# Layer norm over channels: 1/std spread by a store and a broadcast load instead of TensorE, its sums in a one-bank PSUM accumulator, and a new table for the planned order

## The chip, the cores and the metric

One NeuronCore of a Trainium2 chip runs the whole program. The metric is the time of one execution on the device in microseconds (us); a figure for a kernel is the median over its runs. TensorE does matmuls, VectorE and ScalarE elementwise work, GpSimd some elementwise work and DMA issues, SyncE only issues DMAs.

## The reference

One layer of a decoder on 1024 tokens of 1024 channels, then a final RMSNorm, all in float32. Cut to what matters:

```python
h = rmsnorm(x, norm_g) * (1.0 + scale) + shift
u = h @ w_in                                   # 5 groups of 1024 columns
cv, cg, cs, lx, ls = split(u)
v = cv * sigmoid(cg)
v = causal_depthwise_conv(v, dw_w, dw_b)       # 31 taps
v = silu(layernorm(v, cln_g, cln_b))           # over the 1024 channels
v = v @ pw2_w + pw2_b
y_conv = v * silu(cs)
...                                            # y_lru from lx, ls: conv, gates, scan
y = concat([y_conv, y_lru]) @ w_out
x = x + (1.0 + gate) * y
return rmsnorm(x, final_g)
```

with `layernorm(v) = (v - mu) * rsqrt(var + eps) * g + b`, where `mu` and `var` are taken over the channels of a token.

## The kernel before, in words

**Layout.** Channels lie on the 128 partitions, in 8 tiles, and the 1024 tokens in the free dimension. So a sum over channels is a sum over the partitions and over 8 tiles, and a number per token (a mean, a 1/std) has to be spread over the partitions before VectorE can use it. A float32 matmul operand is split into a high and a low part in the type fp32r, and a product is three matmuls of 128x512: `uh,whi`, `ul,whi` and `uh,wlo` (`mm_k`, line 739). Where two column tiles or two row tiles are taken together, sums and differences of their blocks save products (`duo` for two tiles of W_in with the accumulators `up` and `dn`; `lru_pair` for two column tiles of W_out with `lx`, `lw`, `lc`, `ld`; `pair_products` for the projection pw2, with `xpw`, `ypw`, `zpw`, and for the rest of W_out, with `xout`, `yout`, `zout`).

**Stages.** RMSNorm of x with the modulation; the 40 column tiles of W_in in the order of the string `ORDER`, with the depthwise convolution of a value tile as soon as that tile is there, and gates and scan of the lru group between; then the lru half of W_out, which needs no layer norm; the layer norm over channels beside it; pw2; the conv half of W_out; the final norm. The conv outputs are eight tiles `c` (four go through DRAM and come back as `cr`), their sum is `csum`.

**The layer norm** (`layer_norm`, line 1735). `csum` is split in `csh` and `csl`, and a matmul with ones spreads the mean over the partitions (`mean`, line 1742). VectorE subtracts the mean from each tile, ScalarE squares it into `lnsq`, VectorE adds the squares up in `lnss`. Then `rstd` (line 957) does three steps: eight matmuls with a column of ones (line 970) sum `lnss` over the partitions into 8 columns of the PSUM tile `lnbc`, token by token down the partitions; ScalarE takes the root (`sd`), VectorE the reciprocal (`rs`, line 987); and eight matmuls with the identity (line 976) turn the 128x8 numbers into a 128x1024 tile in which every partition has every token's 1/std. VectorE multiplies each tile by `lnbc` out of PSUM, ScalarE applies scale, bias and Silu. VectorE and ScalarE then make the operands of pw2 out of them: `vha`, `vhb`, `vhc` and `vhT` are high parts of tiles, sums and differences, `vla`, `vlb` and so on their low parts. The weights of pw2 come as `rawpw` loads on SyncE's queue and are split into `whipw`, `wlopw`, `h34pw`, `l34pw`, `hlpw`.

**What sets the order.** Every instruction is handed to a planner (`Plan`, line 334) with its engine, a cost, a priority and the tiles that it reads and writes. `Plan.order` walks through time with these costs, takes for each free engine the ready operation with the smallest priority whose tiles are to be had, and so fixes the order on each engine; `Plan.run` adds to the priorities the numbers of the table `TURNS`, which name an engine, the first and the last tile of an operation and its count:

```python
seen[key] = n = seen.get(key, -1) + 1
o.prio += TURNS.get((*key, n), 0.0)
out = self.order()
```

The engines run their lists in order. SyncE's list is the queue of the ordinary loads and stores, so a DMA that waits for its data holds up all DMAs behind it. Constants choose who does a piece of work: `WE` and `DENG` give the low parts of weights to VectorE, GpSimd or a DMA that adds, `CENG` sums of the convolution, `LRV` the remainders of the lru weights.

**Memory.** 47 big tiles of 128x1024 in SBUF; two each of the weight tiles `raw`, `whi`, `wlo`; in PSUM three tiles `mm` of two banks and two tiles `acc` of one bank (128x512). `lnbc` and `mean` are `mm` tiles, and so are the accumulators of the W_in and W_out products.

Of the kernel before, what the change touches and what calls it, by code (L numbers as in the profile page):

```python
# [34 lines left out]
ORDER = "i10 i24 i2 g0 i25 i11 i3 i26 i33 i12 i4 g1 i34 i23 g2 i13 i35 i5 i27 g3 i20 i14 i39 i6 i28+i36 i15 i30+i38 i7 i29+i37 g5 i31 g4 i19 i18+i22 g6 i21 g7"  # L35
# [12 lines left out]
HRES = 2  # L48
# [42 lines left out]
KQ = 0.5  # L91
# [64 lines left out]
LRV = (0, 1, 2, 3, 4, 5, 6)  # L156
# [19 lines left out]
WE = {5: "POOL", 6: "DMA", 7: "DVE", 8: "POOL", 9: "POOL", 10: "DVE", 11: "POOL", 12: "POOL", 13: "POOL", 14: "DMA", 16: "POOL", 18: "DVE", 19: "DVE", 20: "DVE", 21: "DVE", 23: "DVE", 24: "DVE", 25: "POOL", 26: "DVE", 27: "POOL", 28: "DMA", 30: "POOL", 31: "DMA", 32: "DMA", 33: "DMA", 34: "DMA", 35: "DVE", 36: "DVE", 37: "DVE", 38: "DVE", 39: "DMA", 40: "POOL", 41: "DVE"}  # L176
PDIRECT = (2, 4, 5, 6, 7)
D1S = {15: -1.35, 18: -1.35, 19: -1.35, 21: -0.3, 22: 0.0, 23: -1.35, 25: -1.35, 26: -1.35, 29: -0.3, 32: -1.35, 33: 0.0, 35: -1.35, 36: -1.35, 38: -1.35, 39: -1.35, 40: 0.0, 41: -1.35}
PGM, PYM, PXL, PYL, PXR = (2, 3), (0, 4), (0,), (4, 6, 7), (4, 6)
# [2044 lines left out]
```

## Time and profile before

| what | before |
|---|---|
| median of 3 runs | 721.93 us (721.25 to 722.73) |
| the profiled execution | 722.32 us, of which the span of instructions 720.5 us |
| TensorE busy | 710.7 us, 99% of the span, 3244 matmul instructions |
| VectorE busy | 642.2 us, 89% |
| ScalarE busy | 475.4 us, 66% |
| GpSimd busy | 217.9 us, 30% |
| DMA | 136.61 MB, mean 190 GB/s |
| mean granted clock of TensorE | 0.996 |

The profiled execution has a time of its own; its span is shorter by what lies ahead of the first and behind the last instruction. A busy share is the time with at least one instruction running on an engine. The matmuls overlap one another: one lasts 389 ns in the records, and the next one starts before it ends, so what a row of matmuls costs is read from start to start. "PE", "DVE", "ACT", "POOL" and "SP" stand for TensorE, VectorE, ScalarE, GpSimd and SyncE; L976 is line 976 of the kernel. An arrow "<-" behind an idle time names what ended it.

### The profile page before, as it was taken

What the parts mean: (1) busy time and instruction counts of PE and PEld (TensorE: products, weight loads), DVE (VectorE), ACT (ScalarE), POOL (GpSimd) and SP (SyncE); (2) the same over time, 40 slices, a digit from 0 to 9 for tenths busy, and PEclk for the clock granted to TensorE, in tenths of its full rate; (3) what the DMA queues carried; (4) which work ended last, traced back from release to release, by engine and by line L of the source; (5) the groups of instructions that cost most, each with busy time, mean ns of one, the idle gap of its engine ahead of it and who ended that gap; (6) DMA issues with size and microseconds to landing.
All of it is one profiled execution on the core that took longest, in us unless ns stands there. A gap on an engine that the chain in (4) does not pass through costs nothing.

```text
span 720.5 us, 9054 instructions
## 1 busy us (share of the span) xinstructions
PE 710.7 (99%) x3244; PEld 591.5 (82%) x3244; DVE 642.2 (89%) x884; ACT 475.4 (66%) x601; POOL 217.9 (30%) x188
## 2 busy tenths in 40 slices
PE   9999999999999999999999999999999999999996
PEld 8888888888888888887788888888888888878885
DVE  7989999899989989969988999999699874998747
ACT  7650699848748865974694979947497654744422
POOL 0023334554765752374163361100111011100001
PEclk9999999999999999999999999999999999999998
DMA  9946358998787999699764339997737855893006
GB/s 336 407 159 192 56 151 198 255 268 184 172 216 198 246 232 230 168 228 200 220 173 117 88 92 275 256 341 196 177 49 151 217 126 129 247 251 116 30 1 233
DMA packets 45196, 136.61 MB, mean 190 GB/s; under 512 B 5104, under 2 KB 14576, under 8 KB 45040
## 3 DMA queue, kind: packets, MB, share of 16 engines
q1 hardware_dynamic: 27440, 90.00, 35.5%
q0 software_dynamic: 16704, 45.13, 35.0%
q10 hardware_dynamic: 1008, 0.92, 0.4%
q8 instruction: 25, 0.41, 0.2%
q14 instruction: 19, 0.16, 0.1%
HBM read 83.30 MB, written 25.69 MB: 151 GB/s over the span
## 4 chain that ended last, share of the span: by engine, by line
PE 84%; DVE 7%; ACT 3%; issue 3%; POOL 2%; DMA 1%; DVEq 0%; POOLq 0%; ACTq 0%
PE ps L747 36%; PE xout L923 5%; PE first L1056 5%; PE xpw L923 5%; PE dn L747 3%; PE lx L1640 3%; PE dn L1851 3%; PE gate L1487 2%; PE ypw L923 2%; PE up L747 2%; DVE caccs L606 1%; PE y L893 1%; DMA wloout<-in_w_out_dram 1%; PE zout L923 1%; PE lx L747 1%
## 5 line engine op out<-in xcount | busy, mean ns | idle before, releaser
L747 PE MATMUL ps<-uh,whi 128*128 128x512 f32 x448 | 138.0, 389 | 0.0
L747 PE MATMUL ps<-uh,wlo 128*128 128x512 f32 x448 | 138.0, 389 | 0.0
L747 PE MATMUL ps<-ul,whi 128*128 128x512 f32 x448 | 137.8, 389 | 0.0
L747 PEld LDWEIGHTS ps<-ul,whi 128*128 128x128 f32 x448 | 84.1, 188 | 17.4
L747 PEld LDWEIGHTS ps<-uh,wlo 128*128 128x128 f32 x448 | 84.1, 188 | 17.4
L747 PEld LDWEIGHTS ps<-uh,whi 128*128 128x128 f32 x448 | 84.0, 188 | 17.4
L606 DVE SCALAR_TENSOR_TENSOR cacc<-v,V,cacc 128x511 f32<-128x511 f32 (+14 forms) x90 | 66.7, 741 | 0.2
L587 ACT CAST whi<-raw 128x1024 fp32r<-128x1024 f32 (+1 forms) x44 | 44.1, 1007 | 33.7 <-issue 11.2
L606 DVE SCALAR_TENSOR_TENSOR caccs<-v,V,caccs 128x511 f32<-128x511 f32 (+6 forms) x84 | 62.5, 744 | 3.7 <-ACT caccs L595 2.8
L606 DVE SCALAR_TENSOR_TENSOR caccs<-c,wsum,caccs 128x511 f32<-128x511 f32 (+6 forms) x84 | 62.4, 743 | 0.7
L614 POOL TENSOR_TENSOR wlo<-raw,whi 128x1024 fp32r<-128x1024 f32 (+1 forms) x16 | 38.6, 2416 | 71.8 <-ACT whi L587 70.1
L595 ACT ACT_TABLE_LOAD x45 | 57.7, 1283 | 3.5 <-DVE r L1499 1.1
L619 POOL DMA_DIRECT2D es<-cq x30 | 28.3, 944 | 27.9 <-DMA es<-cq 11.8
L606 DVE SCALAR_TENSOR_TENSOR modw<-modw,sc 128x1024 f32<-128x1024 f32 x23 | 32.4, 1412 | 0.2 <-DMA modw<-in_mod_w_dram 0.2
L614 DVE TENSOR_TENSOR wlo<-raw,whi 128x1024 fp32r<-128x1024 f32 (+1 forms) x22 | 28.7, 1306 | 2.0 <-ACT whi L587 2.0
L619 POOL DMA_DIRECT2D oo<-co x26 | 26.1, 1067 | 14.4 <-issue 5.5
L595 ACT ACTIVATE cq<-v,V 128x511 f32<-128x511 f32 (+14 forms) x30 | 21.1, 711 | 13.6 <-DVE modw L606 6.5
L619 POOL DMA_DIRECT2D accd<-acc x8 | 7.0, 874 | 72.9 <-ACT acc L595 51.4
L614 POOL TENSOR_TENSOR o<-fin,bc 128x256 f32<-128x256 f32 (+1 forms) x6 | 4.9, 836 | 70.9 <-ACT bc L587 70.9
L595 ACT ACTIVATE finsq<-fin 128x512 f32<-128x512 f32 (+2 forms) x14 | 7.9, 571 | 27.0 <-DVE fin L606 14.8
L619 POOL DMA_DIRECT2D lz<-in_w_out_dram x16 | 14.1, 948 | 37.2 <-ACT lz L595 32.8
L606 DVE SCALAR_TENSOR_TENSOR xs<-ps,V,xs 128x1023 f32<-128x1023 f32 (+2 forms) x15 | 19.2, 1278 | 4.2 <-ACT xs L595 4.1
(523 smaller groups left out, 1928.6 us busy)
## 6 DMA issues: line engine op xcount, KB each, us to landing
raw<-in_w_in_dram SPq DMA_DIRECT2D x36, 512.0 KB, 4.8
modw<-in_mod_w_dram SPq DMA_DIRECT2D x24, 512.0 KB, 8.4
scsd<-scs SPq DMA_DIRECT2D x8, 512.0 KB, 3.6
raw<-in_w_out_dram SPq DMA_DIRECT2D x8, 512.0 KB, 5.2
accd<-acc POOLq DMA_DIRECT2D x8, 512.0 KB, 5.9
rawpw<-in_pw_dram SPq DMA_DIRECT2D x8, 512.0 KB, 4.6
scsr<-scsd SPq DMA_DIRECT2D x8, 512.0 KB, 5.6
rawout<-in_w_out_dram SPq DMA_DIRECT2D x8, 512.0 KB, 4.0
```

What stands on the lines that cost most here:

```text
L587: act.copy(out(), in_())
L595: act.activation(out=out(), in_=in_(), func=func, **kw)
L606: dve.scalar_tensor_tensor(out=out(), in0=in0(), scalar=scalar, in1=in1(), op0=op0, op1=op1, accum_out=accum)
L614: lambda: e.tensor_tensor(out=out(), in0=a(), in1=b(), op=op), prio, r, w,
L619: return S.op("POOL", ISSUE, lambda: pool.dma_start(out(), a(), accum_op=ALU.add), prio, r, w, lag=RATE * n / T, after=after, flight=flight)
L747: pe.matmul(ps()[:, a - off:b - off], k3(lhs)()[:, at, :], rhs[k]()[:, a:b], start=(k == first and lhs is wh and rhs is xh and (a - off) % ...
L893: pe.matmul(to(), half(*lhs)()[:, j * P:j * P + P], half(*rhs)()[:, c0:c1], start=a == "S1" and j == 0 and t == 0, stop=j == KT // 2 - 1 a ...
L923: pe.matmul(half(ps, 0)(), half(*lhs)()[:, j * P:j * P + P], half(*rhs)(), start=start and at == 0 and i == 0, stop=at == len(order) - 1 a ...
L1056: pe.matmul(ps()[:, a - off:b - off], fw_part(lhs, k, i * P, i * P + P)(), rhs()[:, a:b], start=k == 0 and lhs is wh and rhs is xh, stop=k ...
L1487: pe.matmul(ps()[:, c0:c1], lhs()[:, j, :], rhs()[:, c0:c1], start=st == 0, stop=st == 2)
L1640: pe.matmul(half(ps, h)(), lhs()[:, o:o + P], half(*rhs)(), start=begin and at == 0 and t == 0, stop=at == len(order) - 1 and t == len(ter ...
L1851: pe.matmul(half(ps, h)(), lhs()[:, o:o + P], half(rhs, z)(), start=begin and j == 0 and t == 0, stop=j == NJ - 1 and t == 2, skip_group_c ...
```

## The change

The layer norm calls a new function instead of `rstd` with `lnbc`:

```diff
-        bc = mm_tile("lnbc")
-        rstd(-1, [ss], 0, T, bc, 0)
+        if LNB == "PE":
+            bc = mm_tile("lnbc")
+            rstd(-1, [ss], 0, T, bc, 0)
+        else:
+            bc = root_rows(ss, o)
```

```diff
+LNB, LNC, LNP, LNS = "DMA", False, 0.5, "acc"
...
+    def root_rows(ss, last_sq):
+
+
+        sums, rs = (acc_tile if LNS == "acc" else mm_tile)("lnsum"), S.buf("rs", "lnrs")
+        row = dram.tile([1, T], F32, tag="lnrow", name="lnrow")
+
+        def stats():
+            for b in range(KT):
+                pe.matmul(sums()[:, b:b + 1], ss().rearrange("p (t b) -> p b t", b=KT)[:, b, :],
+                          ones[:, 0:1], start=False, stop=True, skip_group_check=True)
+        TS(-1, lambda: sums()[:, :KT], lambda: ones[:, :KT], 0.0, None, ALU.mult, w=[sums], after=[last_sq])
+        S.op("PE", 0.224 * KT, stats, -1, [ss], [sums])
+        ACT(-1, lambda: rs()[:, :KT], lambda: sums()[:, :KT], AF.Sqrt, KT, bias=eps_t, scale=1.0 / D,
+            r=[sums], w=[rs])
+        S.op("DVE", 0.2, lambda: dve.reciprocal(rs()[:, :KT], rs()[:, :KT]), -1, [rs], [rs])
+        DMA(LNP, lambda: row[0].rearrange("(p b) -> p b", b=KT), lambda: rs()[:, :KT], P * KT * 4,
+            r=[rs], w=[("lnrow", 0)])
+        wide = big_buf("lnwide")
+        DMA(LNP, wide, lambda: row.to_broadcast([P, T]), FULL_BYTES, r=[("lnrow", 0)], w=[wide])
+        if not LNC:
+            return wide
...
```

So the eight matmuls of the sums write into a one-bank accumulator (`lnsum`, zeroed by VectorE, then added to), with every eighth token in a column instead of 128 tokens in a row, so that the 8 numbers of a partition lie side by side in memory. Root and reciprocal work in one tile `lnrs`. SyncE stores its 128x8 numbers into a row of 1024 in DRAM (`lnrow`, 32 bytes from each partition) and loads that row into every partition of the SBUF tile `lnwide`. VectorE multiplies by `lnwide` from SBUF. The eight matmuls with the identity are gone.

Beside it the tables that set the order are new: `TURNS` grows from 117 entries to 951, `ORDER` swaps some slots, and a few constants move single pieces of work:

```diff
-ORDER = "i10 i24 i2 g0 i25 i11 i3 i26 i33 i12 i4 g1 i34 i23 g2 i13 i35 i5 i27 g3 i20 i14 i39 i6 i28+i36 i15 i30+i38 i7 i29+i37 g5 i31 g4 i19 i18+i22 g6 i21 g7"
+ORDER = "i10 i24 i2 g0 i25 i11 i3 i26 i33 i12 i4 g1 i34 i23 g2 i13 i35 i5 i27 g3 i20 i39 i14 i6 i28+i36 i15 i30+i37 i7 i29+i38 g4 g5 g6 i31 i19 i22+i18 g7 i21"
...
-LRV = (0, 1, 2, 3, 4, 5, 6)
+LRV = (0, 1, 2, 4, 5, 6)
...
 TURNS = {
...
-    ("ACT", "c1", "cq1_14", 0): -8,
-    ("ACT", "c3", "vhb1", 0): -1.7,
+    ("ACT", "", "", 1): -0.2,
+    ("ACT", "c1", "cq1_10", 0): 0.8,
...
```

(`i` is a column tile of W_in, `+` a duo, `g` a pair of gates of the lru group.) Other constants of the same kind that differ: `HRES`, `KQ`, `DENG`, `EVD`, `DUOE`, `PRES`, `PREP`, `XCP`, `HSP`, `CENG`, `LWO`, `WE`, `PDIRECT`, `D1S`, `PYL`. Over the whole program, TensorE's matmuls of 128x512, 128x256 and 128x1 are the same in number, and those of 128x128 are 8 fewer.

**TensorE at the sums and the spread.** The rows of `lru_pair` on both sides are products of W_out (`yh`, `yl`: lru outputs, `whi`, `wlo`, `lsh`, `lsl`: weights). Before:

```order
L1640 MATMUL lx_4221<-yhs_3858,lsl_4076 128x512
L970 MATMUL lnbc<-ones,lnss 128x1 x8
L747 MATMUL lw_4230<-yh_3368,whi_4155 128x512
L747 MATMUL lw_4230<-yl_3383,whi_4155 128x512
L747 MATMUL lw_4230<-yh_3368,wlo_4163 128x512
L747 MATMUL lw_4230<-yh_3864,whi_4155 128x512
L747 MATMUL lw_4230<-yl_3883,whi_4155 128x512
L747 MATMUL lw_4230<-yh_3864,wlo_4163 128x512
L976 MATMUL lnbc<-ident,rs-1_0_4285 128x128 x8
L1640 MATMUL lx_4221<-yhs_3908,whi_4155 128x512
```

and in the changed kernel:

```order
L2475 MATMUL lc_4251<-yh_3812,whi_4172 128x512
L2475 MATMUL lc_4251<-yl_3859,whi_4172 128x512
L2475 MATMUL lc_4251<-yh_3812,wlo_4212 128x512
L2578 MATMUL lnsum<-ones,lnss 128x1 x8
L2475 MATMUL lc_4251<-yh_3780,whi_4172 128x512
L2475 MATMUL lc_4251<-yl_3790,whi_4172 128x512
L2475 MATMUL lc_4251<-yh_3780,wlo_4212 128x512
```

The sums stand 9 matmuls of 128x512 sooner in TensorE's list, and behind them the W_out products go on with no spread in between.

**VectorE from the last sums of squares to the first product.** `lnss` is the running sum, `ld` and `lw` are sums of W_out blocks in PSUM with a copy `lk`. Before:

```order
L614 TENSOR_TENSOR lnss<-lnss,lnsq_4192 128x1024
L614 TENSOR_TENSOR ld_4253<-lx_4221,lk_4244 128x512
L614 TENSOR_TENSOR lnss<-lnss,lnsq_4219 128x1024
L614 TENSOR_TENSOR lw_4230<-lx_4221,lk_4244 128x512
L987 RECIPROCAL rs-1_0_4285<-sd-1_0_4283 128x8
L614 TENSOR_TENSOR c_3289<-c_3289,lnbc 128x1024
```

and in the changed kernel:

```order
L1463 TENSOR_SCALAR lnsum<-ones 128x8
L1449 TENSOR_TENSOR lnss<-lnss,lnsq_4119 128x1024
L1449 TENSOR_TENSOR lnss<-lnss,lnsq_4189 128x1024
L1449 TENSOR_TENSOR lnss<-lnss,lnsq_4214 128x1024
L1449 TENSOR_TENSOR wlo_4272<-raw_4191,whi_4257 128x1024
L2584 RECIPROCAL lnrs<-lnrs 128x8
L1449 TENSOR_TENSOR ld_4290<-lx_4237,lk_4235 128x512
L1449 TENSOR_TENSOR lw_4219<-lx_4237,lk_4235 128x512
L1449 TENSOR_TENSOR c_2349<-c_2349,lnwide 128x1024
L1449 TENSOR_TENSOR cr_3984<-cr_3984,lnwide 128x1024
```

The zeroing of `lnsum` stands three additions ahead of the sums; the remainder of a W_out weight (`wlo`) and the piece `ld` have come between the last `lnss` and the products, which read `lnwide`.

**SyncE's queue.** `raw` are weights of W_out, `rawpw` those of pw2. Before:

```order
L633 DMA raw_4174<-in_w_out_dram 128x1024
L633 DMA raw_4201<-in_w_out_dram 128x1024
L633 DMA rawpw_0_4371<-in_pw_dram 128x1024
L633 DMA rawpw_1_4386<-in_pw_dram 128x1024
L633 DMA rawpw_0_4581<-in_pw_dram 128x1024
```

and in the changed kernel:

```order
L1468 DMA raw_4191<-in_w_out_dram 128x1024
L1468 DMA lnrow<-lnrs 128x8
L1468 DMA lnwide<-lnrow 128x1024
L1468 DMA rawpw_0_4355<-in_pw_dram 128x1024
L1468 DMA rawpw_1_4358<-in_pw_dram 128x1024
L1468 DMA rawpw_0_4540<-in_pw_dram 128x1024
```

Store and broadcast load stand between the last `raw` and the first `rawpw`, so all loads of pw2's weights are issued behind them.

**TensorE at the start of pw2.** In the changed kernel:

```order
L1582 MATMUL lc_4369<-yh_3828,whi_4257 128x512
L1582 MATMUL lc_4369<-yl_3847,whi_4257 128x512
L1582 MATMUL lc_4369<-yh_3828,wlo_4272 128x512
L1758 MATMUL xpw_0_4531<-vha_4363,whipw_4439 128x512
L1758 MATMUL xpw_0_4531<-vha_4363,wlopw_4455 128x512
L1758 MATMUL xpw_0_4531<-vha_4521,whipw_4439 128x512
L1758 MATMUL xpw_0_4531<-vha_4521,wlopw_4455 128x512
L1582 MATMUL ld_4411<-yh_3371,whi_4257 128x512
```

Before, the 12 products of `ld` with this weight stood ahead of the first `xpw`; now they stand between the first products of pw2, three at a time at first.

## Rows read from the trace of the kernel before

**Rows 1.** The page: busy time; TensorE and its granted clock in 40 slices, in tenths.
```profile
PE 710.7 (99%) x3244; PEld 591.5 (82%) x3244; DVE 642.2 (89%) x884; ACT 475.4 (66%) x601; POOL 217.9 (30%) x188
...
PE   9999999999999999999999999999999999999996
...
PEclk9999999999999999999999999999999999999998
```

**Rows 2.** Waits of PE: who waited for whom, total us, times, longest us.
```profile
PE lx L1640 <- ACT acc L595: 0.4, 1, 0.4
PE xout L923 <- DMA wloout<-in_w_out_dram: 0.4, 1, 0.4
PE dn L1851 <- DVE dn L614: 0.4, 1, 0.4
PE dn L1851 <- ACT up L587: 0.3, 1, 0.3
```

**Rows 3.** Timeline of PE, 507.5 to 508.8 us: start, duration, instruction.
```profile
507.79 0.39 PE L747 MATMUL lx<-yh,wlo 128*128 128x512 f32 x1
508.58 0.50 PE L1640 MATMUL lx<-yh,whi 128*128 128x512 f32 x1 [0.40 <-ACT acc L595]
```

**Rows 4.** The chain that ended last, 486 to 525 us: start, duration, what.
```profile
514.32 1.36 PE lx L1640 x6
515.67 1.68 PE lnbc L970 x16
...
518.87 1.78 PE lnbc L976 x16
520.65 1.39 PE lx L1640 x6
```

**Rows 5.** Timeline of DVE, 513 to 522 us, with idle time ahead.
```profile
513.67 1.22 DVE L614 TENSOR_TENSOR lnss<-lnss,lnsq 128x1024 f32<-128x1024 f32 x1
...
517.69 0.20 DVE L987 RECIPROCAL rs-1_0_4285<-sd-1_0_4283 128x8 f32<-128x8 f32 x1 [1.28 <-ACT sd-1_0_4283 L595]
520.69 2.35 DVE L614 TENSOR_TENSOR c<-c,lnbc 128x1024 f32<-128x1024 f32 x2 [2.79 <-PE lnbc L976]
```

**Rows 6.** Timeline of ACT, 513 to 526 us.
```profile
517.39 0.27 ACT L595 ACTIVATE sd-1_0_4283<-lnbc,eps_t 128x8 f32<-128x8 f32 x1 [3.31 <-PE lnbc L970]
...
521.95 2.38 ACT L595 ACTIVATE c<-c,V 128x1024 f32<-128x1024 f32 x2 [2.98 <-DVE c L614]
```

**Rows 7.** DMA issues: times, KB each, median us to landing.
```profile
rawpw<-in_pw_dram SPq DMA_DIRECT2D x8, 512.0 KB, 4.6
...
rawout<-in_w_out_dram SPq DMA_DIRECT2D x8, 512.0 KB, 4.0
...
lsdl<-ll SPq DMA_DIRECT2D x4, 512.0 KB, 7.1
...
lsl<-lsdl SPq DMA_DIRECT2D x4, 512.0 KB, 7.3
...
out_dram<-o SPq DMA_DIRECT2D x9, 128.0 KB, 2.4
```

**Rows 8.** Timeline of SP's queue, 500 to 560 us.
```profile
509.23 39.27 SPq L633 DMA_DIRECT2D rawpw<-in_pw_dram  x3
```

**Rows 9.** Timeline of PE, 553.1 to 553.3 us.
```profile
552.95 0.39 PE L747 MATMUL ld<-yh,wlo 128*128 128x512 f32 x1
553.17 0.39 PE L923 MATMUL xpw<-vha,whipw 128*128 128x512 f32 x1
```

**Rows 10.** Groups of ACT, 521 to 553 us, by shape: busy us, mean ns.
```profile
L595 ACT ACTIVATE cr<-cr,V 128x1024 f32<-128x1024 f32 x4 | 5.0, 1238 | 0.0
...
L587 ACT CAST vhb<-c 128x1024 fp32r<-128x1024 f32 x3 | 3.1, 1045 | 0.0
...
L587 ACT CAST vha<-cr 128x512 fp32r<-128x512 f32 x3 | 1.8, 628 | 0.0
```

**Rows 11.** Timeline of POOL, 630 to 646 us.
```profile
634.48 0.86 POOL L619 DMA_DIRECT2D wloout<-in_w_out_dram  x1 [4.08 <-ACT wloout L595]
```

More of the change, by code (lines that the diff above doesn't have):

```diff
@@ new lines @@
+    ("ACT", "cacc6", "c6", 0): -0.7,
+    ("ACT", "caccs2", "c2", 0): -1,
+    ("ACT", "caccs7", "c7", 0): -1,
+    ("ACT", "cr0", "lnss", 0): 0.9,
+    ("ACT", "cr0", "vha0", 0): -5,
+    ("ACT", "cr1", "vhb0", 0): 1.7,
+    ("ACT", "cr2", "lnsq2", 0): -1.6,
+    ("ACT", "cr2", "vha1", 0): 4.3,
+    ("ACT", "cr4", "vha2", 0): 6,
+    ("ACT", "dn27", "up27", 0): -0.1,
+    ("ACT", "dn37", "scs2", 0): 0.1,
+    ("ACT", "dn37", "wk37", 0): -1.6,
+    ("ACT", "first_u0", "first_u0", 0): 6.4,
+    ("ACT", "fraw2", "fhi2", 0): -1,
@@ new lines @@
+    ("DVE", "c3", "lnwide", 0): 0.2,
+    ("DVE", "c3", "mean", 0): -10.2,
+    ("DVE", "c3", "oo3", 0): -11.5,
+    ("DVE", "c3", "oo3", 1): -2.3,
+    ("DVE", "c3", "vlb1", 0): 1,
+    ("DVE", "c3", "vu1", 0): 3.5,
+    ("DVE", "c4", "caccs4", 0): -0.2,
+    ("DVE", "c4", "caccs4", 1): -0.1,
+    ("DVE", "c4", "caccs4", 2): 0.8,
+    ("DVE", "c4", "caccs4", 6): -0.2,
+    ("DVE", "c4", "caccs4", 9): -0.5,
+    ("DVE", "c4", "caccs4", 10): 0.1,
+    ("DVE", "c4", "caccs4", 11): 0.1,
+    ("DVE", "c4", "caccs4", 13): -0.2,
@@ new lines @@
+    ("DVE", "c5", "caccs5", 14): 1.3,
+    ("DVE", "c5", "caccs5", 15): -5.8,
+    ("DVE", "c5", "caccs5", 16): -1,
+    ("DVE", "c5", "lnwide", 0): -1.5,
+    ("DVE", "c5", "mean", 0): -3.5,
+    ("DVE", "c5", "vlb2", 0): 0.2,
+    ("DVE", "c5", "vt2", 0): -1.8,
+    ("DVE", "c5", "vt2", 1): -0.1,
+    ("DVE", "c6", "cacc6", 0): -1.6,
+    ("DVE", "c6", "caccs6", 2): -0.1,
+    ("DVE", "c6", "caccs6", 4): 0.5,
+    ("DVE", "c6", "caccs6", 6): 2,
+    ("DVE", "c6", "caccs6", 8): -0.3,
+    ("DVE", "c6", "caccs6", 9): 1.6,
@@ new lines @@
+    ("DVE", "c7", "mean", 0): -0.4,
+    ("DVE", "c7", "vlb3", 0): 11.7,
+    ("DVE", "c7", "vt3", 0): 0.3,
+    ("DVE", "c7", "vt3", 1): 0.2,
+    ("DVE", "c7", "vu3", 0): 3.4,
+    ("DVE", "cr0", "mean", 0): -0.9,
+    ("DVE", "cr0", "vu0", 0): -2,
+    ("DVE", "cr1", "lnwide", 0): 0.3,
+    ("DVE", "cr1", "mean", 0): -0.8,
+    ("DVE", "cr1", "vt0", 0): -8.9,
+    ("DVE", "cr2", "mean", 0): -1.5,
+    ("DVE", "cr2", "vu1", 0): 6.8,
+    ("DVE", "cr4", "lnwide", 0): 2,
+    ("DVE", "cr4", "mean", 0): 1.4,
@@ new lines @@
+    ("DVE", "graw1", "glo1", 0): -0.1,
+    ("DVE", "graw2", "glo2", 0): -0.2,
+    ("DVE", "graw7", "glo7", 0): -0.1,
+    ("DVE", "lnss", "lnsq2", 0): -2,
+    ("DVE", "lnsum", "lnsum", 0): 0.1,
+    ("DVE", "lx3", "ld3", 0): -1,
+    ("DVE", "lx3", "lw3", 0): 5.8,
+    ("DVE", "modw1", "sc", 0): 0.3,
+    ("DVE", "modw11", "sc", 0): -2,
+    ("DVE", "modw19", "sc", 0): -0.3,
+    ("DVE", "ps13", "xs2", 1): 0.1,
+    ("DVE", "ps13", "xs2", 2): 0.3,
+    ("DVE", "ps21", "v5", 0): 0.3,
+    ("DVE", "ps22", "xs3", 2): -0.4,
@@ new lines @@
+    ("POOL", "ylc1", "yt1", 0): -4,
+    ("SP", "", "", 0): 3.9,
+    ("SP", "", "", 1): -0.2,
+    ("SP", "", "", 2): 1.5,
+    ("SP", "", "", 4): -0.3,
+    ("SP", "", "", 5): -0.2,
+    ("SP", "", "", 8): 0.2,
+    ("SP", "c0", "c0", 0): 1.8,
+    ("SP", "c2", "c2", 0): 0.3,
+    ("SP", "cr1", "cr1", 0): -0.1,
+    ("SP", "graw4", "graw4", 0): 0.1,
+    ("SP", "lnwide", "lnwide", 0): -1.7,
+    ("SP", "lsh0", "lsh0", 0): 0.1,
+    ("SP", "lz0", "lz0", 0): 2,
+    ("SP", "lz2", "lz2", 0): -2.7,
```

955 lines of the change are left out of this document (854 added, 101 removed).

## The prediction, made before the changed kernel ran

> **What bounds the kernel now.** I read the busy line first, then the waits of TensorE, the chain of waits, the timelines of VectorE, ScalarE and SyncE's queue around the layer norm, and the table of DMA issues. TensorE is busy 710.7 us of a span of 720.5 us, 99%, the tenths show a 9 in every slice but the last, and its granted clock reads 9 in all slices but the last [rows 1]. VectorE with 89% is close behind, ScalarE and GpSimd are not. So the time is the number of TensorE instructions by their spacing, plus its few holes: six matmuls of 512 columns take 1.36 us in the chain [rows 4], 0.2267 us each. In its waits I count four in the middle of the program: `lx` for ScalarE's `acc`, `xout` for the load of `wloout`, and two of `dn`, together 1.5 us [rows 2]. From start to start the holes are longer: at `lx` two matmuls start 0.79 us apart, at 507.79 and 508.58 [rows 3], which is 0.56 more than the spacing, and the next one comes 0.11 late. The four are alike, 2.5 us in all. Everything that VectorE, ScalarE and the DMAs do counts only where it makes such a hole.
>
> The chain shows the stage that is changed [rows 4]: the sums of the squares over the partitions (16 instructions of line 970, 1.68 us), six matmuls for W_out, then the spread of 1/std (16 instructions of line 976, 1.78 us), and TensorE goes on with W_out without a hole. Beside it VectorE finishes the last `lnss` at 514.9, makes the reciprocal at 517.69 after 1.28 us of idling, and idles 2.79 us more until `lnbc` is spread, so the first product with it starts at 520.69 [rows 5]; ScalarE's root starts at 517.39 and its first Silu at 521.95 [rows 6]. The first matmul of the pw2 projection comes at 553.17, on the spacing, and waits for nothing [rows 9].
>
> **The change, part by part.** *Removed: the spread.* 8 matmuls of 128x128 are 16 instructions and take 1.78 us [rows 4], all on the path, since TensorE's rows around them are dense. The matmuls of every other shape are the same in number in both orders, so this is the only thing that TensorE does less: **-1.78 us**. The 8 sums stay, at 1.68 us [rows 4].
>
> *Added on VectorE: zeroing 8 columns of the accumulator*, the shape of the reciprocal, 0.20 us [rows 5]; one whole-tile remainder more and a three-quarter one less add about 0.1 to 0.2 us. The cover: VectorE idles 1.28 and 2.79 us in this stage [rows 5], so it costs nothing; if that idle time were gone, it would be 0.2 us later at the first product. Root and reciprocal now share one buffer, which costs nothing.
>
> *Moved: the sums come sooner.* Between the csum and the last `lnss`, VectorE's order holds 21.5 us of work at the row durations where it held 24.0 (fewer remainders of W_out and combinations of `lx` and `lk` stand between). The csum keeps its time (1.3 us more ahead of the last value tile, 1.3 less behind it). So the last `lnss`, which began at 513.67 and took 1.22 [rows 5], ends at about 511.6 instead of 514.9. TensorE comes to the row of the sums, at 515.67 before [rows 4], with nine matmuls fewer ahead of it: at 513.6, or at 511.5 if the three holes before it close. I reckon with the latter; with the former, all that follows here and TensorE's arrival at pw2 shift alike. Sums 1.68 [rows 4], root 0.27 [rows 6], reciprocal 0.20 [rows 5], with the steps between: 1/std is there at 511.6 + 1.7 + 0.3 + 0.3 = 513.9.
>
> *Added: the trip through DRAM.* Nothing like it is in the trace: the store is 4 KB, 32 bytes a partition. Its nearest rows are the smallest stores, 128 KB of the output in 2.4 us, and the largest of the slow ones, `lsdl`, in 7.1 us. The load brings 512 KB into SBUF; such loads from DRAM take 4.0 us (`rawout`) to 7.3 us (`lsl`) [rows 7]. I take 2.4 us for the store, as it is a small one and SyncE's queue is quiet here, and 4.8 for the load, near the 4.6 us of `rawpw`, the loads that follow on the same queue. The trip is then 7.2 us, with ends at 6.4 and 14.4, and `lnwide` is there at 521.1, against 520.69 for the first product now. So the products come no sooner, although the sums come 3.3 us sooner: the trip eats it all. VectorE waits about as long as before (its two pieces `ld` and `lw` and a remainder stand between the reciprocal and the first product), and a product with an SBUF operand takes what it takes with PSUM: the additions to `lnss`, all SBUF, last 1.22 us each, and two products 2.35 [rows 5].
>
> The Trainium skill, page "DMA: Bandwidth & Descriptors", section "Anatomy of one DMA — SWDGE (gpsimd) path", gives a DMA a fixed 2.0 us, mostly the receipt of the last write, and the rest by bytes; by that, as an estimate, store and load would be 2.0 and 3.2 us, 5.2 together, and `lnwide` there at 519.1. The loads of this trace, 4.0 us and more, do not agree with the 3.2, and the sum stays with the rows.
>
> *Who waits for it.* On SyncE's queue the store waits for the reciprocal and the load for the store; behind them stand all eight `rawpw` loads and the `scsr` ones. In the trace the first three `rawpw` loads are issued from 509.23 us on [rows 8]; they would move to about 516.5 and land 4.6 us later [rows 7], at 521 to 522. Their first readers are casts on ScalarE 14 and 15 rows behind the first Silu, some 12 us, at about 534. That costs nothing; with a trip of 14.4 they land at 526, still in time.
>
> *What stands on the end of the path: the pw2 matmuls.* In the new order TensorE comes to the first of them sooner: the spread (1.78 us) is gone, and 12 matmuls of `ld` (2.72 us) that stood ahead of it stand between its pieces. With the holes as they are, that is 553.17 - 4.50 = 548.7; with all holes before it closed, 546.5. Its inputs come from ScalarE: from the first Silu to the cast `vha1` there are 28 rows: seven Silu at 1.13 us apart, eight of 1024 columns at 0.96 apart, thirteen of 512 at 0.52 to 0.6, about 22.8 us (one lasts 1.24, 1.05 and 0.62 [rows 10], but the next begins before its end). First product at 521.1, first Silu 1.26 later as before, `vha1` at 545.2. That is 1.3 us ahead of the earliest arrival of TensorE, 3.5 ahead of the other. VectorE's `vla` of this stage have 1.2 to 1.4 us by the same reckoning. So no hole, but the slack is thin: each us of the trip beyond about 8.5 can become a us of TensorE.
>
> *The order elsewhere.* The replaced table moves rows on every engine; the work is the same but for one remainder by DMA instead of GpSimd. It matters only at the four holes. At two of them the W_in pieces `dn` stand elsewhere now, with a gate or another piece in between; at `lx` the neighbours differ too. The load of `wloout` (issued at 634.48 [rows 11], landed 8.7 us later) is the exception: TensorE's place where it is needed is 2.5 us sooner in time, so that hole can stay or grow. I take about 1 us of the 2.5 as gone, **-1.0 us**, ends 0 and -2.5, and above it +1 for new holes.
>
> Sum: -1.8 - 1.0 = -2.8. The profiled execution took 722.32 us; 719.5 for the changed one. The median of the runs is 721.93, 0.39 below, so **719.2 us** for the median.
>
> **The rivals.** *A: the spread goes, the holes stay.* For it: a replaced order has its own late pieces, and `wloout` was late before. Then 721.93 - 1.78 = 720.15, with new holes of up to 1.5 us 721.6. *B: all four holes close:* 721.93 - 1.78 - 2.5 = 717.65, and with the small excesses beside them, 0.9 us more, 716.7. Against it: `wloout`. *C: slower, the trip is late.* The place is the wait of VectorE's first product for `lnwide`; behind it stand all products, Silu and casts, and then pw2. The point is a trip of 8.5 us; at the bounds, 7.1 + 7.3 = 14.4 [rows 7], TensorE stands still for 5.9 us, and 721.93 - 2.8 + 5.9 = 725.0. From a trip of 11.3 us it is slower than before, from 12.7 by more than can be told; at 10 it is 720.6. For it: no store in pieces of 32 bytes is in the table of issues, and if such a store takes as long as the slowest there, 7.1 us, it is 719.2 + 3.4 = 722.6 with an ordinary load; I give that 0.06 of C's chance. For it too: the three `rawpw` loads go out right behind the load and share the engines with it. Against it: nothing stands ahead of the two on their queue at that time, and 12.7 us needs both near their worst rows.
>
> The Trainium skill, same page, section "Specifications", has the DMA engines read and write back where pieces are below 512 bytes. That would speak for the slow store of C; no run so far shows it.
>
> *D: the order does harm elsewhere*, for instance a W_out load that comes 4 us later than its place, 723.5 or more; nothing in the profile picks such a place.
>
> **How the numbers follow.** The forecast (718.4 to 720.4) has 0.50, B 0.12, A 0.18, C 0.15, D 0.05. The measurement of this kernel can tell about 0.2%, 1.44 us, from no change, so faster is below 720.5 and slower above 723.4. Faster: 0.50 + 0.12 + 0.07 of A (its 720.15 lies close to the edge) = 0.69. Slower: 0.08 of C and 0.03 of D = 0.11. Same: the rest, 0.20. The range goes from the bound of B, 716.7, to 723.2, where a trip of about 12.5 us would end; it leaves out most of the slower cases and the low tail, less than 0.2.
>
> **What would show it.** In the changed profile: 2 x 8 instructions of TensorE fewer; the sums at 511 to 512; the store in 2 to 3.6 us and the load in 4 to 5.5; the first product at 520 to 522; the first pw2 matmul at 546.5 to 548 without a wait for ScalarE or VectorE; TensorE's waits in the middle down from four to two or so. The forecast is wrong if `lnwide` comes after 523 and pw2 waits, or if TensorE's waits elsewhere add up to more than 2.5 us.

## The result and the profile after

The changed kernel takes 724.87 us (median of 20 runs, 722.9 to 728.5) where the kernel before, on the same chips, takes 722.82 (20 runs, 721.25 to 723.4): a ratio of 1.0035, 95% interval 1.0023 to 1.0047. It is slower by 0.35%, where 719.2 us, 0.4% less than the 721.93 us before, was forecast; the time lies outside the range, and none of the rivals named the reason. The profiled execution took 725.22 us, its span is 723.3. In the first experiment below one execution took 1025.88 us at a mean granted clock of 0.655; it is counted in that kernel's median of 721.29 us (721.19 without it) and in no ratio.

The page after, busy time by engine, against [rows 1]:

```profile
span 723.3 us, 9041 instructions
...
PE 712.6 (99%) x3228; PEld 592.9 (82%) x3228; DVE 644.1 (89%) x885; ACT 477.1 (66%) x603; POOL 218.9 (30%) x188
```

The 16 instructions of the spread are gone (3244 to 3228), and yet TensorE is busy 1.9 us longer. The stage shows why. TensorE's timeline around the sums (start, duration, instruction):

```profile
513.64 0.40 PE L2475 MATMUL lc<-yh,wlo 128*128 128x512 f32 x1
513.87 3.74 PE L2578 MATMUL lnsum<-ones,lnss 128*128 128x1 f32 x16
517.47 0.77 PE L2475 MATMUL lc<-yh,whi 128*128 128x512 f32 x1
518.03 0.63 PE L2475 MATMUL lc<-yl,whi 128*128 128x512 f32 x1
518.46 0.63 PE L2475 MATMUL lc<-yh,wlo 128*128 128x512 f32 x1
...
520.98 0.39 PE L2475 MATMUL lx<-yhs,lsl 128*128 128x512 f32 x1
521.21 0.40 PE L1582 MATMUL lc<-yh,whi 128*128 128x512 f32 x1
```

The sums take 3.6 us from start to start, where the same 16 instructions took 1.68 [rows 4]. Behind them, matmuls of 512 columns start 0.43 us apart instead of 0.2267 [rows 4]: from 517.47 to 521.21 there are nine, in 3.74 us, which should have taken 2.04. The view by stretches (busy time of TensorE, granted clock, DMA share, GB/s) says what these 1.7 us are:

```profile
504.00:513.90 9.90, 9.90 (x46) 1.00 0.80 160
513.90:517.50 3.60, 3.60 (x18) 1.00 0.66 119
517.50:521.00 3.50, 3.50 (x10) 0.51 0.14 18
521.00:526.00 5.00, 5.00 (x23) 1.00 0.90 302
```

Behind the sums TensorE is granted half its clock, 1.2 GHz instead of 2.4, for some 3.5 us. By the profile it was busy all the time from 504 us on; just ahead of the fall it had done nothing but one-column matmuls for 3.6 us. In the kernel before the clock was 1.00 in the same stretches (busy time of TensorE, its weight loads, VectorE, ScalarE and GpSimd, then clock, DMA share, GB/s):

```profile
513.90:517.50 3.60, 3.60 (x25) 3.29 (x24) 1.69 (x2) 0.29 (x2) 0.90 (x1) 1.00 0.95 244
517.50:521.00 3.50, 3.50 (x25) 3.15 (x24) 0.52 (x2) 1.44 (x2) 0.00 (x0) 1.00 0.61 108
```

Why the sums are slow stands in the view of their tile (durations in ns: least, median, most):

```profile
L2578 PEld LDWEIGHTS lnsum<-ones,lnss x16: 316/335/336, 513.6 to 517.2; 128*128 128x128 f32 x16
L2578 PE MATMUL lnsum<-ones,lnss x16: 171/376/377, 513.9 to 517.2; 128*128 128x1 f32 x16
```

and in the kernel before, for the same instructions:

```profile
L970 PEld LDWEIGHTS lnbc<-ones,lnss x16: 187/192/192, 515.3 to 517.1; 128*128 128x128 f32 x16
```

`lnss` is the weight of these matmuls, and each load takes 335 ns instead of 192. What differs about the weight is how it is read: `rearrange("p (t b) -> p b t")[:, b, :]` takes every eighth number, 32 bytes apart, where `a + b * P` took 128 in a row. (The sums also go to another PSUM tile; the first two experiments separate the two.) The other waits of TensorE, against [rows 2]:

```profile
PE zout L1758 <- DMA wloout<-in_w_out_dram: 0.8, 1, 0.8
PE lw L1582 <- DMA wlo<-in_w_out_dram: 0.7, 1, 0.7
PE dn L2714 <- DVE dn L1449: 0.5, 1, 0.5
```

From start to start, and with the slower first matmul behind each, all holes between 57 and 690 us make 3.6 us where I had counted 2.5. The account of the profiled execution: -1.78 (spread) + 1.9 (sums) + 1.7 (clock) + 1.1 (holes) = +2.9, and 725.22 - 722.32 is 2.90. That is the account of one execution on each side; the medians of 20 runs lie 2.05 us apart.

### The profile page after: what moved, and what is told of

Same layout as the page of the kernel before. It is cut to its first block, busy times and chain, and to the rows that moved or that the text cites. A ratio compares the mean times of both kernels' runs of the same rounds, so it can differ in the third digit from the quotient of the medians.

```text
span 723.3 us, 9041 instructions
## 1 busy us (share of the span) xinstructions
PE 712.6 (99%) x3228; PEld 592.9 (82%) x3228; DVE 644.1 (89%) x885; ACT 477.1 (66%) x603; POOL 218.9 (30%) x188
## 4 chain that ended last, share of the span: by engine, by line
PE 79%; DMA 6%; issue 5%; DVE 4%; ACT 3%; POOL 2%; DVEq 0%; SPq 0%; POOLq 0%; ACTq 0%
PE ps L1582 34%; PE xout L1758 6%; PE first L1891 5%; PE xpw L1758 5%; PE dn L2714 3%; PE ypw L1758 3%; PE gate L2322 3%; PE dn L1582 2%; PE up L1582 2%; PE lx L2475 2%; PE y L1728 1%; DMA yl<-yr 1%; DMA wlo<-in_w_out_dram 1%; DMA wloout<-in_w_out_dram 1%; PE zpw L1758 1%
## 5 line engine op out<-in xcount | busy, mean ns | idle before, releaser
L1449 POOL TENSOR_TENSOR wlo<-raw,whi 128x1024 fp32r<-128x1024 f32 (+1 forms) x15 | 36.3, 2425 | 72.0 <-ACT whi L1422 70.0
L1449 DVE TENSOR_TENSOR wlo<-raw,whi 128x1024 fp32r<-128x1024 f32 (+1 forms) x22 | 30.5, 1388 | 2.2 <-ACT whi L1422 2.2
L1430 ACT ACTIVATE uh<-x,shift 128x512 fp32r<-128x512 f32 x16 | 10.5, 713 | 23.9 <-PE ps L1582 23.9
```

What stands on the lines that cost most here:

```text
L1430: act.activation(out=out(), in_=in_(), func=func, **kw)
L1449: lambda: e.tensor_tensor(out=out(), in0=a(), in1=b(), op=op), prio, r, w,
```

## The experiments

Theory S: the 32-byte stride makes the sums slow, and the long stretch of one-column matmuls sends the clock down. Rival P: the clock falls because of the new place of the sums, behind a hole, with no W_out products between sums and spread. Rival T: the loss is in the trip through DRAM and its queue. Rival D: the new order itself is the loss. Each run is compared with runs of the kernel before on the same chip.

### The stride alone undone

```diff
-                pe.matmul(sums()[:, b:b + 1], ss().rearrange("p (t b) -> p b t", b=KT)[:, b, :],
+                pe.matmul(sums()[:, b:b + 1], ss()[:, b * P:b * P + P],
```

> The changed kernel with one thing undone: the eight sums read their weights as 128 tokens in a row again instead of every eighth token, in the same order on every engine (the 1/std numbers then go to other tokens, so this computes another layer norm; the work is the same). Theory S (the stride): a weight of single numbers 32 bytes apart loads in 335 ns instead of 192, so the 16 instructions of the sums take 3.6 us instead of 1.7, and that long stretch of one-column matmuls is what sends the granted clock down behind it for 3.4 us, 1.6 us more. Then the sums take 1.7 us here, the clock stays at 1.00 throughout, and the time is 724.9 - 1.9 - 1.6 = 721.4 us (720.6 to 722.0). Rival P (the place): the clock falls because the sums now stand without the W_out products and the spread near them and soon behind a hole of 0.9 us; then the sums take 1.7 us, the clock still falls behind them, 723.0 us. Rival T (the trip through DRAM and the queue): the loss has nothing to do with the sums, 724.9 us within 0.7.

721.29 us against 723.11, ratio 0.9970 (0.9957 to 0.9982). The sums' loads are back, and the clock holds (the tile's view and the stretches of this run):

```profile
L2578 PEld LDWEIGHTS lnsum<-ones,lnss x16: 186/192/192, 516.8 to 518.5; 128*128 128x128 f32 x16
```

```profile
514.00:518.50 4.50, 4.50 (x30) 1.00 1.07 195
518.50:522.00 3.50, 3.50 (x18) 1.00 0.30 63
```

With not one instruction moved, the change goes from 0.35% slower to 0.3% faster. S is borne out, and P, T and D fall as the cause of the loss: place, trip and order are all still there. The difference of the two ratios is 0.65%, 4.7 us; the profile of the changed kernel accounts for 3.6 of it. Its runs differ in what the clock takes: nine of the 20 have a mean granted clock of 0.994 or less, and their median is 726.5 us, that of the other eleven 724.1; here none of the runs compared is below 0.996. That this is the rest of the 4.7 us is likely, but not shown. (This run's profiled execution is the longest of those compared, 724.88 us; it has 2.2 us of holes between 277 and 293 us, at operands of W_in and the gates that came late, far from the layer norm.)

### The stride alone put into the kernel before

```diff
-                pe.matmul(ps()[:, o + b:o + b + 1], sq()[:, a + b * P:a + b * P + P],
+                pe.matmul(ps()[:, o + b:o + b + 1], sq().rearrange("p (t b) -> p b t", b=KT)[:, b, :] if prio == -1
+                          else sq()[:, a + b * P:a + b * P + P],
```

> The kernel before with one thing added: the eight sums read every eighth token as in the change (the spread 1/std then belong to other tokens; the work is the same), same order on every engine. Theory S: the sums take 3.6 us instead of 1.7, +1.9 us, and the clock falls behind them or at the spread, +1.6 us or a little more: 722.8 + 1.9 + 1.6 = 726.3 us (724.5 to 727.5). Rival P: the sums take 3.6 us but here W_out products stand around them, the clock stays at 1.00, 724.7 us. Rival T: no change, 722.8 us.

727.05 us against 723.11, ratio 1.0041 (1.0022 to 1.0060). The loads take 335 ns here too, and the clock falls, 1.4 us behind the sums, so that the whole spread runs at half clock and takes 3.3 us instead of 1.78 (stretches of TensorE; the third is the spread):

```profile
516.30:519.90 3.60, 3.60 (x17) 1.00 0.83 187
519.90:521.40 1.50, 1.50 (x7) 0.95 0.02 4
521.40:524.70 3.30, 3.30 (x18) 0.50 0.00 0
524.70:530.00 5.30, 5.30 (x26) 1.00 0.00 0
```

Old place, old order, spread by TensorE, no trip: the read alone costs this kernel 0.41%, about what the whole change lost. P falls a second time, since W_out products stand between sums and spread here. Two of its seven runs, with a mean clock of 0.998, took 724.2 and 724.6 us, the other five 726.6 to 727.8: by these the clock seems not to fall in every execution.

### Sums twice as long without a stride

```diff
+            for b in range(KT):
+                pe.matmul(sums()[:, KT + b:KT + b + 1], ss()[:, b * P:b * P + P],
+                          ones[:, 0:1], start=False, stop=True, skip_group_check=True)
```

> The changed kernel with sums that read 128 numbers in a row, and taken twice (the second eight into columns that nobody reads; 1/std goes to other tokens as in the plain undo). 32 instructions of one column in about 3.4 us, with no strided load. If the clock falls because of the length of the stretch with hardly any columns (theory S in its second half): the sums take 3.4 us or more, the clock is at half speed for some 3.4 us behind them, 721.4 + 1.7 + 1.6 = 724.7 us. If it is the strided read itself that sends the clock down: no fall, 723.1 us. Rival T: 724.9 + 1.7 = 726.6 us.

725.42 us against 723.11, ratio 1.0027 (1.0011 to 1.0044). 32 one-column instructions with loads of 192 ns, and behind them:

```profile
513.50:517.20 3.70, 3.70 (x34) 0.96 0.65 122
517.20:520.30 3.10, 3.10 (x8) 0.50 0.05 5
520.30:526.00 5.70, 5.70 (x26) 1.00 0.84 274
```

So the clock falls without the strided read too, and TensorE has no hole in the 20 us ahead. It fell behind 3.6 us of such matmuls with loads of either kind, and not behind 1.7 us of them, in any profile here. The stride costs twice because it makes the stretch long.

### The tokens put right by ScalarE, by the store, by VectorE

The stride has a purpose: it puts the eight numbers of a partition in the order of the tokens, so that the store writes 32 bytes at once. Three kernels read the sums in a row and put the tokens right elsewhere, the order of every engine unchanged. By ScalarE, whose eight squares are written in 512-byte steps:

```diff
-                o = ACT(pr, q, c[t], AF.Square, r=[c[t]], w=[q])
+                o = ACT(pr, lambda q=q: q().rearrange("p (b t) -> p t b", b=KT), lambda t=t: c[t]().rearrange("p (t b) -> p t b", b=KT),
+                        AF.Square, r=[c[t]], w=[q])
```

> The changed kernel with the sums reading 128 numbers in a row, and ScalarE writing each square so that every eighth token lies in a row already (the computation is the reference's). Theory S: as in the run with the plain undo, 721.4 us, as long as the squares with 512-byte steps on the write side last 1.05 us as before; if they last up to 1.7 times as long (the stretch that the weight load shows), the last sum of squares comes up to 3 us later, the products too, and the time is up to 2 us more, 723.4. Rival P: 723.0 us and the clock falls. Rival T: 724.9 us.

By the store:

```diff
-        DMA(LNP, lambda: row[0].rearrange("(p b) -> p b", b=KT), lambda: rs()[:, :KT], P * KT * 4,
+        DMA(LNP, lambda: row[0].rearrange("(b p) -> p b", p=P), lambda: rs()[:, :KT], P * KT * 4,
```

> The changed kernel with sums that read 128 tokens in a row, and a store that puts the tokens right: each of the 1024 numbers goes to its own place of the row in DRAM, in pieces of 4 bytes, where the change stores 32 bytes from each partition. Same order on every engine. Theory S: the sums take 1.7 us, the clock stays at 1.00, and the store alone decides. In the run with the plain undo the load landed 0.6 us ahead of the first product and the products had some 2 us in hand before pw2. So a store of up to 3.5 us (1.4 there) costs nothing, 721.3 us; one of 7 us (the slowest store in the trace of before) delays the products by 5 us, and pw2 waits 3 us: 724.5. Theory T (the trip decides): 724 us or more even with a short store, since the plain undo was then only lucky in other respects.

By VectorE, in the last addition of squares:

```diff
+                    TT(pr, "DVE", lambda: sp_().rearrange("p (b t) -> p t b", b=KT), lambda: s0().rearrange("p (t b) -> p t b", b=KT),
+                       lambda q=q: q().rearrange("p (t b) -> p t b", b=KT), ALU.add, r=[s0, q], w=[sp_])
```

> The changed kernel with sums that read 128 numbers in a row; the tokens are put right by VectorE, whose last addition of squares writes into another tile with every eighth token in a row (512-byte steps). Same order, one tile more. Theory S: the sums take 1.7 us, the clock stays up. ScalarE's squares with such steps took 2.05 us instead of 1.05; if VectorE's addition doubles too, from 1.2 to 2.3 us, the sums come 1.1 us later, which is what they waited for TensorE's place in the changed kernel: 721.3 to 722.4 us. If the step costs VectorE nothing: 721.3. Theory T: 724.9.

All three lose what the undo had won. ScalarE: 729.28 us against 723.11, ratio 1.0076 (1.0054 to 1.0097). Its squares take twice as long (they were 1.05 us each), the sums of squares come late, and TensorE waits 3.4 us for an evacuation that stands behind them on ScalarE; behind that hole the clock is at half for 3.4 us. The tile's view of the squares:

```profile
L1430 ACT ACTIVATE lnsq<-c x4: 1989/2076/2115, 495.7 to 513.9; 128x1024 f32<-128x1024 f32 x4
```

and TensorE's longest wait:

```profile
PE lx L2475 <- ACT acc L1430: 3.4, 1, 3.4
```

The store in pieces of 4 bytes: 730.53 us against 722.70, ratio 1.0099 (1.0074 to 1.0125). Here the trip decides. SyncE's queue and VectorE's first product with `lnwide` (timelines):

```profile
514.72 0.38 SPq L1468 DMA_DIRECT2D lnrow<-lnrs  x1
523.22 0.33 SPq L1468 DMA_DIRECT2D lnwide<-lnrow  x1
```

```profile
529.11 1.22 DVE L1449 TENSOR_TENSOR c<-c,lnwide 128x1024 f32<-128x1024 f32 x1 [7.97 <-DMA lnwide<-lnrow]
```

TensorE's longest wait, and its stretches:

```profile
PE lx L2475 <- ACT acc L1430: 5.7, 1, 5.7
```

```profile
526.00:532.20 6.20, 0.52 (x3) 0.83 0.76 248
532.20:536.40 4.20, 4.17 (x10) 0.50 0.00 0
```

The load is issued 8.5 us behind the store, 7.1 us later than in the changed kernel (1.44). And the place where that reaches TensorE is not pw2, as my rival C had it, but W_out: an accumulator of `lx` is read by ScalarE in a row behind the first Silu, so TensorE stands still for it at 526, 5.9 us, and then runs at half clock. By these numbers the slack of the trip there is only 7.1 + 1.6 (the load, 5.9 us instead of 4.3 in the plain undo) - 5.9 = 2.8 us.

VectorE: 723.36 us against 722.70, ratio 0.9999 (0.9984 to 1.0015). One addition takes 1.99 us instead of 1.22, TensorE waits for it ahead of the sums (the tile's view, then TensorE's waits):

```profile
L1449 DVE TENSOR_TENSOR lnsp<-lnss,lnsq x1: 1993/1993/1993, 512.4 to 512.4; 128x1024 f32<-128x1024 f32 x1
```

```profile
PE lnsum L2578 <- DVE lnsp L1449: 0.6, 1, 0.6
```

From start to start that hole is 0.8 us, of the 2 us that it is above the plain undo. In the profiled execution the clock stays at 1.00 behind this hole and the 1.7 us of sums, which speaks against P once more. Five of the twelve runs have a mean clock of 0.995 or less, so it may fall there in some executions; no profile shows that, and where the rest of the 2 us goes stays open.

### The new tables without the trip, and the trip with the old tables

```diff
-LNB, LNC, LNP, LNS = "DMA", False, 0.5, "acc"
+LNB, LNC, LNP, LNS = "PE", False, 0.5, "acc"
```

> The changed kernel with its new order tables but the old way: sums in a row into the two-bank tile, spread by eight matmuls with the identity, no trip through DRAM (the planner shifts some instructions to fit). Theory S: what the change lost is the strided sums and the clock, and its saving is the spread; so this is 721.3 (the plain undo) + 1.8 for the spread = 723.1 us (722.3 to 724.0), with the clock at 1.00. Theory T (trip): without the trip the loss goes and the new order's gain shows, 720.5 or less. Theory D (the new order is the loss): 724.9 or more.

737.12 us against 722.70, ratio 1.0186 (1.0162 to 1.0210).

```diff
-        bc = mm_tile("lnbc")
-        rstd(-1, [ss], 0, T, bc, 0)
+        bc = root_rows(ss, o)
```

> The kernel before with its own order tables and only the layer norm exchanged: sums in the one-bank accumulator with 128 tokens in a row (1/std goes to other tokens), store, broadcast load, products from SBUF; both DMAs are planned ahead of the other loads. Theory S: the spread's 1.8 us saved and nothing else: 722.9 - 1.8 = 721.1 us, if the planner's order around it leaves pw2 its slack. Theory T: pw2 waits for the products, since before's order starts them at 520.7 and the trip of 5.8 us comes after sums that begin only at 515.7: first product at 523.5 or later, 1 to 3 us of TensorE idle at pw2, 722 to 724 us.

727.78 us against 722.70, ratio 1.0069 (1.0047 to 1.0091). Neither came near what was expected, and neither tells the theories apart: in both the planner made another order around the exchanged piece, hundreds of rows differ, and TensorE waits in new places. In the second, VectorE waits 1.8 us for `lnwide` and pw2 then waits for operands, as T had it; behind these holes the clock is at half for 6.8 us (SyncE's queue, and TensorE's longest wait):

```profile
517.25 0.33 SPq L634 DMA_DIRECT2D lnrow<-lnrs  x1
520.29 0.33 SPq L634 DMA_DIRECT2D lnwide<-lnrow  x1
```

```profile
PE zpw L924 <- ACT vhb L588: 2.5, 2, 1.8
```

The store's step is longer here, too: 32-byte pieces as in the changed kernel, but the load is issued 3.04 us behind the store instead of 1.44. The DMA engines were fully busy with other transfers when this store was issued (share 1.07 from 517.2 to 518 us, against 0.14 in the changed kernel's trace from 517.5 to 521); that this is the reason is not shown. What the two runs do show is that layer norm and table belong together: the trip is hidden in the order that was planned for it, and not in the one before. What the new order is worth by itself stays open.

### The sums turned round

If the block of squares streams through TensorE and a weight with a single column of ones picks the row, the sums of a block's 128 tokens come out side by side in one partition. No stride, 8 rows of 128 for root and store, and 128 columns a matmul:

```diff
+    pick = const.tile([P, 2 * KT - 1], F32, tag="pick", name="pick")
+    pool.memset(pick, 0.0)
+    pool.memset(pick[:, KT - 1:KT], 1.0)
...
-                pe.matmul(sums()[:, b:b + 1], ss().rearrange("p (t b) -> p b t", b=KT)[:, b, :],
-                          ones[:, 0:1], start=False, stop=True, skip_group_check=True)
+                pe.matmul(sums()[:KT, :P], pick[:, KT - 1 - b:2 * KT - 1 - b], ss()[:, b * P:b * P + P],
+                          start=b == 0, stop=b == KT - 1, skip_group_check=True)
```

> The changed kernel with the sums turned round, same order on every engine: the block of 128 tokens streams through TensorE (128 columns, read in a row) against a weight of 8 columns of which one is ones, so that the sums of block b land in row b of an 8x128 piece of PSUM, and root, reciprocal and store work on 8 rows of 128 (the store is 8 pieces of 512 bytes, and the tokens are in their places). Theory S: eight matmuls of 128 columns take what the spread took, 1.8 us; no strided load; the granted clock stays at 1.00; the trip is as long as in the change, 5.9 us: 721.3 us as in the plain undo (720.6 to 722.4), below the kernel before. If the clock falls all the same, 723 us; if the store from 8 partitions takes longer than 2.3 us, ScalarE's evacuations behind the first Silu come late and TensorE waits as it did with the store of single numbers.

721.45 us against 723.11, ratio 0.9973 (0.9957 to 0.9988). In this kernel and the two that build on it the first sum opens the accumulation anew, which changes part of another product's; the instructions are the same. Two more pieces were tried on it. The second W_out remainder of the last projection by an engine (one entry less in `DMAW`):

> As the run with the sums turned round, and the second of the two W_out remainders that come as a DMA in the last projection is made by an engine instead (the planner shifts some 25 TensorE instructions behind it). It asks what the late load of this remainder costs the changed kernel, whose profile shows a hole of 1.1 us there and that of before one of 0.6. If the hole goes and nothing takes its place: 721.3 - 1.1 = 720.2 us. If VectorE, which has the work now, is late instead: no gain, 721.3 us or up to 1 us more.

721.51 us, ratio 0.9978 (0.9961 to 0.9995): the wait for `wloout` is gone, one of 0.5 us for VectorE's `fin` has come soon behind it, no gain. And the remainder of one lru column by VectorE again (`LRV` as before):

> As the run with the sums turned round, and the remainder of one lru column of W_out made by VectorE again as before, not by a DMA (the planner shifts some 85 TensorE instructions). The profile of the changed kernel has a hole of 1.0 us at that DMA, those of the undo runs had none. If the hole is there in most runs: 721.3 - 1.0 = 720.3 us. If it was one run's: 721.3 us; VectorE's 1.2 us more work ahead of the sums may delay them by as much, and the hole ahead of the sums is the one thing that brings the clock down: up to 723.5 us.

725.73 us, ratio 1.0026 (1.0010 to 1.0041): a miss, by another way than I had named. The sums and the clock behind them are as in the run before, but TensorE waits at pw2, for `vha` and `vla` 1.2 and 1.1 us, and the clock falls there for 3.4 us. So a hole ahead of the sums is not the one thing that brings it down, as I had written. The slack at pw2 is thin, as the prediction had it.

The last run adds to a zeroed piece, with the whole computation as in the reference:

```diff
+                          start=False, stop=True, skip_group_check=True)
+        TS(-1, lambda: sums()[:KT, :P], lambda: ones[:KT, :P], 0.0, None, ALU.mult, w=[sums], after=[last_sq])
```

> The sums turned round once more (weight of 8 columns, tokens streaming in a row, root and reciprocal on 8 rows of 128), now added to an 8x128 piece that VectorE has zeroed, so that no other accumulation in that bank's partitions is touched and the whole computation is the reference's; same order on every engine. VectorE zeroes 8x128 instead of 128x8, about 0.1 us longer, three additions ahead of the sums and off the path. Theory S: 721.4 us as the run before it (720.6 to 722.2), 0.2% to 0.3% below the kernel before on the same chip, clock at 1.00 at the sums and behind them. If the opening of the bank by the first sum had itself saved something: 722.5 us or more.

721.81 us against 723.69, ratio 0.9974 (0.9961 to 0.9988): faster than the kernel before by 0.26%, and so than the changed one. The tile's view and the stretches:

```profile
L2581 PEld LDWEIGHTS lnsum<-lnss,pick x16: 86/90/91, 514.5 to 516.1; 128*8 128x8 f32 x16
L2581 PE MATMUL lnsum<-lnss,pick x16: 272/273/275, 514.6 to 516.2; 128*8 128x128 f32 x16
```

```profile
510.00:514.60 4.60, 4.60 (x22) 1.00 1.07 196
514.60:516.50 1.90, 1.90 (x18) 1.00 1.02 180
516.50:520.00 3.50, 3.50 (x16) 1.00 0.17 33
```

## Why the prediction was wrong, point by point

- **"Removed: the spread, -1.78 us"** agrees with the runs. With the stride undone the kernel is 1.8 us below the one before (721.29 against 723.11), turned round 1.7 and 1.9. These differences also hold what the new order gains or loses elsewhere, which no run separates.
- **"The 8 sums stay, at 1.68 us" is the step that failed.** I took the row of the old instructions for the new ones, since number, shape and type are the same, and told in my own text of the change that a column holds every eighth token without pricing what that does to the weight's read. They took 3.6 us, 1.9 more. And because the sums stood in the sum as a known row, they got no bounds and no rival.
- **The clock** was read as 9 in all slices but the last [rows 1] and left out. I did not ask what TensorE would be doing for a few microseconds on end in the new stage. It cost 1.7 us more in the profile, and the doubled sums show that this second half of the loss needs no stride.
- **"The sums come sooner"**: by less than forecast. The last `lnss` ended at 512.8, not at about 511.6 (my own 24.0 - 21.5 us give 512.4 rather than 511.6), and TensorE came to the sums at 513.87, as with the holes left as they were (513.6), not at 511.5.
- **"The trip: 7.2 us, ends 6.4 and 14.4"** was too long. The store of 32-byte pieces and the issue behind it take 1.44 us, the load 4.4, 5.8 together. SyncE's queue in the changed kernel, and the load's time to landing from its tile's view:

```profile
518.18 0.32 SPq L1468 DMA_DIRECT2D lnrow<-lnrs  x1
519.62 0.32 SPq L1468 DMA_DIRECT2D lnwide<-lnrow  x1
```

```profile
DMA to landing us min/median/max: 4.4/4.4/4.4
```

  It started late, at 518.18 instead of 513.9, because the sums were late and slow. `lnwide` landed at 519.62 + 4.4 = 524.0, and the first product came at 526.13 without waiting for it: VectorE's list has `ld` and `lw` ahead of the products, and those waited for TensorE's `lx`, which came late behind the slow sums and the half clock:

```profile
521.40 0.70 DVE L1449 TENSOR_TENSOR ld<-lx,lk 128x512 f32<-128x512 f32 x1 [3.25 <-PE lx L2475]
525.52 0.70 DVE L1449 TENSOR_TENSOR lw<-lx,lk 128x512 f32<-128x512 f32 x1 [3.42 <-PE lx L2475]
526.13 1.22 DVE L1449 TENSOR_TENSOR c<-c,lnwide 128x1024 f32<-128x1024 f32 x1
```

- **"No hole at pw2"** was right: the first matmul of pw2 comes at 552.69 in the chain, on the spacing. TensorE came there 4 to 6 us later than the 546.5 to 548.7 that I had worked out, so the changed kernel did not test the slack; that it is thin shows in the run with one remainder more for VectorE, where pw2 waits.
- **"About 1 us of the holes gone"** was wrong: 3.6 us in the changed kernel's profile against 2.5. One of them, 1.0 us at a remainder that now comes by DMA, is not in the profiles of the undo runs. The wait for `wloout` grew, as the prediction feared, from 0.6 to 1.1 us.
- **Rival C** had the right sign for the wrong reason, and the wrong place: in the changed kernel's order a late trip (the store in pieces of 4 bytes) stops TensorE first at a W_out accumulator whose reader stands behind the first Silu on ScalarE, not at pw2.

The Trainium skill has the rule that I missed, on the page "SBUF — State Buffer", section "Door 1: The DMA port swizzle (why `[64,N]` ≈ `[32,N]`)": SBUF has lines of 16 bytes, and an access that crosses to a new line each time pays for it, so that float32 may be strided up to 4 for free. The runs agree at the strides tried, 8 numbers for the weight load (335 against 192 ns) and 128 for ScalarE's and VectorE's writes (2.05 against 1.05 us, 1.99 against 1.22 us); no run tried one of 4 or less.

The prediction weighed two more of its rules. The Trainium skill, page "DMA: Bandwidth & Descriptors", section "Anatomy of one DMA — SWDGE (gpsimd) path", gives the fixed 2.0 us for DMAs that GpSimd issues. On SyncE's queue the store and its wait took 1.44 us in the changed kernel and 3.04 us in the run with the old tables. The Trainium skill, page "DMA: Bandwidth & Descriptors", section "Specifications", has pieces below 512 bytes read and written back. No run separates that at 32 bytes (1.44 and 3.04 us, against 1.28 us with eight pieces of 512 in the last run); with 1024 pieces of 4 bytes the step took 8.5 us, but the number of pieces changed too.

## What to carry to other kernels

An operand with the same shape is not the same instruction: when a change rearranges an access, look at the step between neighbouring numbers, on every engine that reads or writes it, and price it as an unknown. When TensorE is the bound, look also at what a stage leaves it to do: here 3.6 us of one-column matmuls cost their own time and, in the profiles, half the clock for another 3.4 us. Put the reordering where data streams anyway: the operand of a matmul that is chosen to stream, and which row the result lands in, were free here, while ScalarE, VectorE and the DMA each paid for it.

## What the runs showed of the hardware that I had not expected

- A weight of 128x128 float32 whose numbers lie 32 bytes apart loads in 335 ns, one that lies in a row in 192; a weight of 8 columns in 90.
- The granted clock fell to half while the profile shows TensorE busy: at the end of 3.6 us of one-column matmuls or 1.4 us behind them, strided (two kernels) or not (one). In the other profiles in which it fell around the layer norm or pw2 it fell at holes, the longest of them 1.3 to 5.9 us from start to start. It stayed at 1.00 behind 1.7 us of one-column matmuls and behind 1.9 us of 128-column ones.
- Once down, it stayed at half for 3.4 us in five profiles (the three with the long sums, ScalarE's and the one with one remainder more for VectorE) and for 6.8 us in three (the 4-byte store and the two with mixed tables).
- A store of 4 KB from 128 partitions let the load behind it go after 1.44 us when it wrote 32 bytes from each in the changed kernel, after 3.04 us when it did so in the order before, beside other transfers, and after 8.5 us when it wrote 4 bytes at a time.
